# A hybrid recurrent and attention trunk on one core: gates one by one, activations read into place, and two products opened before the last K tile

## The chip, the cores and the metric

The kernel runs on one core of one Trainium2 chip. The metric is the device time of one execution in microseconds (us), the median over the runs; lower is better. A profile shows one execution of its own.

## The reference

The reference is one inference step of a trunk of two layers over 640 tokens: 512 of a prompt and 8 sequences of 16 new ones. Each layer works on a normalised stream, shifted and scaled by a projection of a conditioning vector (adaLN), and adds its output, normalised again and gated, to the stream. Layer 0 is a recurrent mixer, layer 1 attention with stick-breaking weights over a key and value shared by all 16 heads and taken from the stream behind layer 0.

```python
D_MODEL, D_RNN, N_HEADS = 2048, 4096, 16
def recurrent_mixer(hn, h0, conv0, w_in, conv_w, conv_b, w_r, b_r, w_i, b_i, lam, w_out):
    xb, zg = jnp.split(hn @ w_in, 2, axis=-1)
    xb, conv_new = causal_conv(xb, conv0, conv_w, conv_b)
    y, hT = rg_lru(xb, h0, w_r, b_r, w_i, b_i, lam)
    return (y * jax.nn.silu(zg)) @ w_out, hT, conv_new
# rg_lru: r, i = sigmoid(block_diag(x, w_r) + b_r), sigmoid(block_diag(x, w_i) + b_i)
#   log_a = -8 r softplus(-lam); a = exp(log_a); u = sqrt(-expm1(2 log_a)) * (i * x); h = a * h + u
def stick_breaking_mixer(hn, k_all, v_all, w_in, w_out):
    q, zg = jnp.split(hn @ w_in, 2, axis=-1)
    o = stick_breaking(q, k_all, v_all)
    return (o * jax.nn.silu(zg)) @ w_out
# each layer: x = x + gate * rms_norm(out, g_post)
```

## The kernel before, in words

All large products are made in float32 precision out of three passes (`mm3`, L99): each operand is split into a high part (`wh`, `yh`, `xh`, `hh`), made on ScalarE (ACT), and a low part (`wl`, `yl`, ...), made on VectorE (DVE) as the difference; then high × high (L101), low × high (L102) and high × low (L103) go into one bank. The split of a weight is `hilo` (L82): L87 on ACT, L88 on DVE, into three buffers of each (`WB`). The names of the profile follow: `wh<-raw` at L87 is the high part of a weight that was loaded into the buffer `raw`.

The tokens lie along the free axis (640, or two halves of 320), 128 features on the partitions. The program goes through these stages:

- *Start* (`start`, L339). For each of 16 K tiles k of the model dimension: four loads of adaLN weights (`wa`), 16 small products with the conditioning vector into a bank (L223), a copy (`msb`, L225), two products with a selector (L228), then the normalised and modulated K tile k (`hn`), split into `xs` or `xv`; `fill(k - 1)` then multiplies the tile before with the first weights (`wf`) of four output tiles, whose sums stay in the banks `psb` and `pss` ("f banks"): 24 matmuls. K tile 15 is filled behind the loop.
- *Pairs* (`recurrent`, L743). 16 pairs of output tiles of the recurrent dimension. Each pair makes two pair products (`pair_product`, L537): the input branch (`inputs`) and the gate branch (`silu_gates`); those of pair 0 come out of the f banks. A pair product multiplies 14 K tiles in two-by-two blocks in the manner of Strassen's method, with seven sums of activations and seven of weights, called S1, X11, S4, S2, X12, S3, X22 in the order of the code; each is 7 × 3 matmuls of 320 columns (21). The last two K tiles (`PLAIN`) go plainly, 6 matmuls for each quarter. Four banks `pc`, `pa`, `pb`, `pd` take them; `keep` (L559) copies a bank to memory on ACT where its intermediate is needed later; `evac` takes the results out on DVE. Weights come by a generator (`plan`, L442, `pair_weights`, L494): loads on SP into `raw`, `rest`, `sum0`, `sum1` and a small ring `rv`, additions of weight blocks by accumulating loads on POOL, and splits, always three weights ahead (`ahead`, L529).
- *Gates and recurrence* (`lru`, L683), once a pair: four products each for the gate r and the gate i, out of the split activation, into four banks (`psg`), a sigmoid on ACT for each (`g` and `q`), then exp, tanh and sqrt on ACT, the products of them on DVE and a scan. The result goes to memory (`yd`).
- *Two out_products* (`recurrent_out`, L854; `out_product`, L761): 16 K tiles of `yd` each, times `w_out_a`; five token blocks by four column blocks. Weights for two K tiles at a time come into a ring of four buffers, `wr`; the activations come into the same ring (`yr`), are split into `yh` and `yl`, and stay.
- *mid* (L909): residual, norm and transposes, interleaved with the end of the second out_product. `residual` (L840) loads the rows of x into `xx`, in two buffers, and adds them (L851).
- *Shared key and value, 16 heads of attention, out_b*: head after head, with the last product (`attention_begin`, L886, `out_product` again, on `od`) started within the last heads; then the last residual.

Each engine works through its queue in order. A scheduler places the instructions into the queues; `issue_after` ties an instruction behind another, and `high_priority` puts it ahead of others that are ready. So what stands in front of a split on ACT or DVE, and in front of a load on SP, decides when it runs.

## Time and profile before

| | before |
|---|---|
| median of 3 runs | 2911.41 us (2906.17 to 2912.74) |
| the profiled execution | 2916.01 us, of it the span 2914.3 us |
| mean granted clock of TensorE | 0.992 |
| instructions | 48223 |
| TensorE busy | 97% of the span |
| VectorE, ScalarE, GpSimd busy | 68%, 55%, 14% |
| bytes moved by DMA | 536.49 MB, 184 GB/s in the mean |

PE stands for TensorE's matmuls, PEld for its weight loads, DVE for VectorE, ACT for ScalarE, POOL for GpSimd, SP for the engine that issues most loads. A row of a timeline gives the start and the duration in us, the engine, the line of the kernel, the instruction, its output and inputs by the program's names, and in square brackets how long the engine was idle before it and who ended that. Where DVE or ACT is named, the waiting engine waited for that instruction's result. An idle time of TensorE costs what it lasts; an idle time of another engine costs only if TensorE waits for it at the end.

### The profile page before, as it was taken

The page shows a single profiled execution, that of the slowest core. Times are in us where ns is not written, and L with a number is a line of the kernel's source. Part 1 is how long each engine was busy: PE and PEld are TensorE (multiplying, and loading weights), DVE is VectorE, ACT ScalarE, POOL GpSimd, SP SyncE. Part 2 cuts the span into 40 slices and gives each one's busy share as a digit, 9 for nine tenths or more (in the row PEclk, how much of TensorE's full clock was granted, in tenths as well). Part 3 has the DMA queues.
Part 4 walks back from the last instruction along what each step waited for, and adds up shares of the span by engine and source line. Part 5 has one row for each costly group of instructions (what it writes and reads, how often), then busy time and mean ns, then how long its engine had stood idle before and what let it go on. Part 6 is the DMA issues. An engine that isn't in the chain of part 4 may idle for free.

```text
span 2914.3 us, 48223 instructions
## 1 busy us (share of the span) xinstructions
PE 2837.1 (97%) x18784; PEld 2520.8 (86%) x18784; DVE 1977.9 (68%) x2867; ACT 1607.8 (55%) x2464; POOL 420.3 (14%) x589
## 2 busy tenths in 40 slices
PE   6899999999999999999999999999999999999998
PEld 4799999999999977778788999778989999897886
DVE  7677776777677766634568877777666766667335
ACT  5466555655565566533456666674455555546323
POOL 0011222222222200001113322001000000001000
PEclk9899999999999999999999999999999999999999
DMA  9866676667666666555567666663565555656636
GB/s 338 303 143 150 162 163 152 146 164 160 158 146 162 143 195 190 167 147 163 186 209 254 226 209 214 203 200 115 185 197 168 182 175 183 198 169 197 208 109 224
DMA packets 246003, 536.49 MB, mean 184 GB/s; under 512 B 22520, under 2 KB 106616, under 8 KB 244624
## 3 DMA queue, kind: packets, MB, share of 16 engines
q1 hardware_dynamic: 219056, 442.01, 47.7%
q0 software_dynamic: 26720, 91.42, 15.5%
q8 instruction: 147, 2.41, 0.3%
q14 instruction: 80, 0.66, 0.1%
HBM read 496.24 MB, written 37.11 MB: 183 GB/s over the span
## 4 chain that ended last, share of the span: by engine, by line
PE 79%; ACT 6%; DVE 4%; DMA 2%; issue 2%; POOL 0%; DVEq 0%; POOLq 0%; SPq 0%; ACTq 0%
PE acc L101 7%; PE acc L102 7%; PE acc L103 7%; PE psh L101 6%; PE acck L101 5%; PE psh L103 5%; PE psh L102 5%; PE acck L103 5%; PE acck L102 5%; PE pa L101 3%; PE pa L103 3%; PE pa L102 3%; PE psa L198 2%; DVE wl L88 1%; PE pc L101 1%
## 5 line engine op out<-in xcount | busy, mean ns | idle before, releaser
L88 DVE TENSOR_TENSOR wl<-wr,wh 128x1024 fp32r<-128x1024 f32 x216 | 270.3, 1252 | 289.4 <-ACT wh L87 288.1
L87 ACT ACTIVATE wh<-wr 128x1024 fp32r<-128x1024 f32 x216 | 228.2, 1056 | 382.1 <-PE acc L103 228.6
L101 PE MATMUL acc<-wh,yh 128*128 128x512 f32 x960 | 378.8, 395 | 10.3 <-ACT yh L777 5.6
L102 PE MATMUL acc<-wl,yh 128*128 128x512 f32 x960 | 378.3, 395 | 7.7 <-DVE wl L88 7.7
L103 PE MATMUL acc<-wh,yl 128*128 128x512 f32 x960 | 377.0, 394 | 0.3 <-DVE yl L778 0.3
L186 DVE TENSOR_TENSOR wa<-wa,wa 128x1024 bf16<-128x1024 f32 (+1 forms) x256 | 308.6, 1240 | 24.9 <-ACT wa L185 22.7
L101 PE MATMUL psh<-nh,wh 128*128 128x320 f32 x1024 | 323.9, 316 | 0.0
L103 PE MATMUL psh<-nh,wl 128*128 128x320 f32 x1024 | 318.9, 311 | 0.0
L102 PE MATMUL psh<-nl,wh 128*128 128x320 f32 x1024 | 317.4, 310 | 0.0
L185 ACT ACTIVATE wa<-wa 128x1024 bf16<-128x1024 f32 x256 | 263.1, 1052 | 67.2 <-DVE wa L186 46.7
L101 PEld LDWEIGHTS acc<-wh,yh 128*128 128x128 f32 x960 | 182.1, 190 | 58.4 <-issue 8.7
L102 PEld LDWEIGHTS acc<-wl,yh 128*128 128x128 f32 x960 | 182.5, 190 | 47.7 <-DVE wl L88 10.3
L103 PEld LDWEIGHTS acc<-wh,yl 128*128 128x128 f32 x960 | 182.2, 190 | 39.9 <-DVE yl L778 2.2
L101 PEld LDWEIGHTS psh<-nh,wh 128*128 128x128 f32 x1024 | 192.3, 188 | 19.3 <-DVE ql L1112 12.6
L101 PE MATMUL pa<-xs,wh 128*128 128x320 f32 x630 | 194.8, 309 | 0.0
L103 PE MATMUL pa<-xs,wl 128*128 128x320 f32 x630 | 194.7, 309 | 0.0
L102 PE MATMUL pa<-xs,wh 128*128 128x320 f32 x630 | 194.7, 309 | 0.0
L103 PEld LDWEIGHTS psh<-nh,wl 128*128 128x128 f32 x1024 | 192.4, 188 | 0.5 <-DVE wl L88 0.2
L102 PEld LDWEIGHTS psh<-nl,wh 128*128 128x128 f32 x1024 | 192.4, 188 | 0.1
L101 PE MATMUL acck<-nh,wh 128*128 128x320 f32 x512 | 161.5, 315 | 0.0
L481 POOL DMA_DIRECT2D sum<-w_in_a_dram x90 | 79.4, 882 | 559.3 <-DVE wl L88 262.9
L103 PE MATMUL acck<-nh,wl 128*128 128x320 f32 x512 | 158.3, 309 | 0.0
(354 smaller groups left out, 7312.4 us busy)
## 6 DMA issues: line engine op xcount, KB each, us to landing
wa<-w_ada_dram SPq DMA_DIRECT2D x192, 512.0 KB, 4.7
wr<-w_out_a_dram SPq DMA_DIRECT2D x96, 512.0 KB, 4.1
sum<-w_in_a_dram POOLq DMA_DIRECT2D x90, 448.0 KB, 5.6
wr<-w_in_b_dram SPq DMA_DIRECT2D x64, 512.0 KB, 5.3
ck<-cache_k_dram SPq DMA_DIRECT2D x64, 512.0 KB, 6.7
cv<-cache_v_dram SPq DMA_DIRECT2D x64, 512.0 KB, 5.3
wr<-w_out_b_dram SPq DMA_DIRECT2D x56, 512.0 KB, 4.2
raw<-w_in_a_dram SPq DMA_DIRECT2D x60, 448.0 KB, 4.2
```

What stands on the lines that cost most here:

```text
L87: nc.scalar.activation(hi[:, :n], raw, AF.Copy)
L88: nc.vector.tensor_tensor(lo[:, :n], raw, hi[:, :n].bitcast(F32), ALU.subtract)
L101: mm(out, sh, mh, start=start, stop=False, **kw)
L102: mm(out, sh, ml, start=False, stop=False, **kw)
L103: mm(out, sl, mh, start=False, stop=stop, **kw)
L185: nc.scalar.activation(parts[i], raw, AF.Copy)
L186: nc.vector.tensor_tensor(parts[2] if i else raw, raw, parts[i], ALU.subtract)
L198: nc.tensor.matmul(ps[32 * j : 32 * j + 32, :], self.c3[:, 4 * g + j, :], ws[j // 2][i][:, j % 2, :], start=g + i == 0, stop=g == 3 and i ...
L481: self.nc.gpsimd.dma_start(self.big[tag], self.quarter(w, i), accum_op=ALU.add)
```

## The change

**The start.** The loads of the adaLN weights are issued ahead of the rest of each step (`ada_load`). In the last step (k = 15) `fill(14)` comes ahead of the last adaLN products instead of behind them. The two banks that adaLN uses are exchanged. The plan of the weights begins in `start`: the first weights are split before the last K tile is made, and the products S1 and X11 of the first pair product are made (`self.opened`, in banks of the ring `one`) between the last selector products and `fill(15)`. `pair_product` takes over from there (`begun`, `opening`). The first loads of the plan come in another order (`raw`, one small one, `rest`, and `sum1` and two small ones later). `lru_params`, small vectors for the recurrence, is made in step 1 instead of at the end.

**The pairs.** `keep` gets high priority. In `lru` the products go gate by gate: r of both halves of the features, then i of both, and after each the weights of that gate are free for the plan (`ahead(1 - i)`); before, both gates of the first half came first. The four banks are taken by half of the features instead of by gate.

**The out_products.** The activations are loaded straight into the tiles that will hold their low parts (`fetch`, four K tiles at a time, the first four before the first weights) and split in place. They use no buffer of the ring `wr` any more. The splits of the first four have high priority. `kept` says which K tiles are still in memory (the last head's, for out_b).

**mid.** `residual` has six buffers for `xx` instead of two.

The number of matmuls is the same. What the change does to the queues, at three places. First PE's queue at the end of the start; `wa` are adaLN's last weights, `psb` and `pss` with `xv` the fills, `sel` the selector products. Before:

```order
L223 MATMUL pss<-wa_1409,cT 32x256 x4
L223 MATMUL pss<-wa_1415,cT 32x256 x4
L101 MATMUL psb<-xv,wh 128x384
L102 MATMUL psb<-xv,wh 128x384
L103 MATMUL psb<-xv,wl 128x384
L228 MATMUL psb<-sel,msb_1421 128x16 x2
L101 MATMUL pss<-xv,wh 128x256
```

And of the change:

```order
L103 MATMUL pss<-xv,wl 128x256
L228 MATMUL pss<-wa_1433,cT 32x256 x4
L228 MATMUL pss<-wa_1435,cT 32x256 x4
L228 MATMUL pss<-wa_1437,cT 32x256 x4
L228 MATMUL pss<-wa_1439,cT 32x256 x4
L234 MATMUL psb<-sel,msb_1481 128x16 x2
L101 MATMUL pc_1519<-xs,wh 128x320
L102 MATMUL pc_1519<-xs,wh 128x320
L103 MATMUL pc_1519<-xs,wl 128x320
```

`fill(14)` (its last row is the first one here) now ends ahead of the adaLN products, and S1 (`pc`) follows the selector, with X11 (`pa`) and `fill(15)` behind it.

Second, PE's queue in the input branch of a pair, behind S4: the end of the plain products (`pd` with `xv`) and what follows them. Before:

```order
L101 MATMUL pd_3109<-xv,wh 128x320
L102 MATMUL pd_3109<-xv,wh 128x320
L103 MATMUL pd_3109<-xv,wl 128x320
L101 MATMUL pb_3108<-xs,wh 128x320
L102 MATMUL pb_3108<-xs,wh 128x320
L103 MATMUL pb_3108<-xs,wl 128x320
```

And of the change:

```order
L101 MATMUL pd_3107<-xv,wh 128x320
L102 MATMUL pd_3107<-xv,wh 128x320
L103 MATMUL pd_3107<-xv,wl 128x320
L101 MATMUL pa_3022<-xs,wh 128x320
L102 MATMUL pa_3022<-xs,wh 128x320
L103 MATMUL pa_3022<-xs,wl 128x320
```

Before, the first half of X12 (`pb`) followed; now S2 (`pa`) does, whole, and X12 behind it.

Third, ACT's queue at the start of the first out_product, from the last sigmoids of the last pair (`g` and `q` from `psg`) to the first split of `wr`. Before:

```order
L702 ACTIVATE g<-psg_11231,pv 128x320
L702 ACTIVATE g<-psg_11239,pv 128x320
L87 ACTIVATE wh<-wr 128x1024
L702 ACTIVATE q<-psg_11248,pv 128x320
L702 ACTIVATE q<-psg_11256,pv 128x320
L712 ACT_TABLE_LOAD
L712 ACTIVATE q<-g,nk_100 128x640 x2
L716 ACTIVATE g<-g,k_99 128x640 x2
L777 ACTIVATE yh<-yr 128x640
```

And of the change:

```order
L751 ACTIVATE q<-psg_11228,pv 128x320
L751 ACTIVATE q<-psg_11236,pv 128x320
L833 ACTIVATE yh<-yl 128x640 x4
L751 ACTIVATE q<-psg_11246,pv 128x320
L751 ACTIVATE q<-psg_11254,pv 128x320
L763 ACT_TABLE_LOAD
L763 ACTIVATE q<-g,nk_100 128x640 x2
L767 ACTIVATE g<-g,k_99 128x640 x2
L87 ACTIVATE wh<-wr 128x1024
```

Four activations are split in the weight's old place, and the weight in the activation's, behind the tanh.

The diff, cut to its core:

```diff
...
-    def ada_first(self, k, psa, psc, dst):
+    def ada_load(self, k):
+        ws = []
+        for g in range(4):
+            ws.append(self.adap.tile([P, 4, 256], F32, tag="wa", name="wa0", bufs=5))
+            self.nc.sync.dma_start(ws[g], self.I["w_ada0"][k, :, 4 * g : 4 * g + 4, :])
+        return ws
+    def ada_first(self, k, ws, psa, psc, dst):
...
         for g in range(4):
-            ws = self.adap.tile([P, 4, 256], F32, tag="wa", name="wa0", bufs=5)
-            nc.sync.dma_start(ws, self.I["w_ada0"][k, :, 4 * g : 4 * g + 4, :])
             for j in range(4):
-                last = nc.tensor.matmul(psa[32 * j : 32 * j + 32, :], self.cT[:, 4 * g + j, :], ws[:, j, :], start=False, stop=g == 3, **kw)
+                last = nc.tensor.matmul(psa[32 * j : 32 * j + 32, :], self.cT[:, 4 * g + j, :], ws[g][:, j, :], start=False, stop=g == 3, **kw)
         m = self.adap.tile([P, 256], F32, tag="msb0", name="msb0", bufs=2)
         nc.scalar.activation(m, psa, AF.Copy)
...
         for i in range(2):
...
         self.ada_put(psc, dst)
         return last.ins
...
             g, s = gs[:, k, :], sh[:, k, :]
-            last = self.ada_first(k, spare[1][:, 256:], spare[0][:, FIRST : FIRST + 32], [self.ada_dst(0, part, k, o) for part, o in ((1, gs), (0, sh))])
+            end = k == KD - 1
+            dst = [self.ada_dst(0, part, k, o) for part, o in ((1, gs), (0, sh))]
+            ada = lambda: self.ada_first(k, ws, spare[0][:, 256:], spare[1][:, FIRST : FIRST + 32], dst)
+            ws = self.ada_load(k)
+            if end:
+                with self.tc.issue_after(last):
+                    last = fill(k - 1)
+                with self.tc.issue_after(last):
+                    last = ada()
+            else:
+                last = ada()
             if k == 0:
...
             self.hT.append((hh, hl))
-            if k > 0:
+            if 0 < k and not end:
                 with self.tc.issue_after(last):
...
             nc.sync.dma_start(raw, self.I["w_first"][:, 4 * P * k : 4 * P * k + 4 * P])
+            if end:
+                self.planned, self.ready = self.plan(), []
+                self.ready.append(next(self.planned))
             wt[k] = self.hilo(raw, P)
+            if k == 1:
+                self.lru_params(rp)
             if k % 2 == 0:
...
                 self.combine(rp, slot, even, tmp)
-        self.lru_params(rp)
-        fill(KD - 1)
+        self.ready.append(next(self.planned))
+        with self.tc.issue_after(last):
+            self.opened = [self.bank(n)[:, :HALF] for n in ("pc7", "pa7")]
+            for ps, i in zip(self.opened, (S1, X11)):
+                last = self.seven(ps, i, True)
+        with self.tc.issue_after(last.ins):
+            fill(KD - 1)
         self.begun = dict(units)
...
         self.smalls = []
-        for _ in range(3):
-            self.small_load()
         at = [w[q] for q in order] + [None, None]
-        for tag, n in (("raw", 0), ("rest", 2), ("sum1", 1)):
-            self.big_load(tag, at[tag == "sum1"], n)
+        self.big_load("raw", at[0], 0)
+        self.small_load()
+        self.big_load("rest", at[0], 2)
         for i, q in enumerate(order):
-            yield from self.pair_weights(*at[i : i + 3], *("sum0", "sum1", "sum0")[i % 2 : i % 2 + 2])
+            weights = self.pair_weights(*at[i : i + 3], *("sum0", "sum1", "sum0")[i % 2 : i % 2 + 2])
+            if i == 0:
+                yield from islice(weights, 2)
+                self.big_load("sum1", at[1], 1)
+                for _ in range(2):
+                    self.small_load()
+            yield from weights
             if q == 1 or q > 16:
...
-    def pair_product(self, ep, evac):
-        nc = self.nc
+    def seven(self, ps, i, first):
+        hi, lo = self.weights()
+        c = slice(HALF * i, HALF * i + HALF)
+        for n, x in enumerate(self.pairs):
+            last = self.mm3(ps, hi[:, n, :], lo[:, n, :], x[:, 0, c], x[:, 1, c], first and n == 0, n == NP - 1, skip_group_check=True)
+        return last
+    def keep(self, ps, tag="keep", bufs=2):
+        t = self.ep.tile([P, HALF], F32, tag=tag, name=tag, bufs=bufs)
+        with self.tc.high_priority(200):
+            self.nc.scalar.activation(t, ps, AF.Copy)
+        return t
+    def opening(self):
+        c, a = self.opened
+        return c, a, self.keep(c, "keep5", 1), self.keep(a)
+    def pair_product(self, evac, begun=None):
         kw = dict(skip_group_check=True)
+        keep = self.keep
...
         def seven(ps, i, first):
-            hi, lo = self.weights()
-            c = slice(HALF * i, HALF * i + HALF)
-            for n, x in enumerate(self.pairs):
-                self.mm3(ps, hi[:, n, :], lo[:, n, :], x[:, 0, c], x[:, 1, c], first and n == 0, n == NP - 1, **kw)
+            self.seven(ps, i, first)
             self.ahead()
...
-        def keep(ps, tag="keep", bufs=2):
-            t = ep.tile([P, HALF], F32, tag=tag, name=tag, bufs=bufs)
-            nc.scalar.activation(t, ps, AF.Copy)
-            return t
-        c, a = bank("pc7"), bank("pa7")
-        seven(c, S1, True)
-        p5 = keep(c, "keep5", 1)
-        seven(a, X11, True)
-        p1 = keep(a)
+        if begun is None:
+            c, a = bank("pc7"), bank("pa7")
+            seven(c, S1, True)
+            p5 = keep(c, "keep5", 1)
+            seven(a, X11, True)
+            p1 = keep(a)
+        else:
+            c, a, p5, p1 = begun
         seven(c, S4, False)
...
-            self.pair_product(ep, evac)
+            self.pair_product(evac, begun)
         return pv, rows
...
         gate_bank = lambda n: self.half(n, "psg2") if n < 2 else self.bank("psg2")
-        rs, qs = [], []
-        for h in range(2):
-            pv = pv2[:, h, :]
-            fs = slice(P * h, P * h + P)
-            g = []
-            for i in range(2):
-                hi, lo = gw[i]
+        gates, qs = [], []
+        for i in range(2):
+            hi, lo = gw[i]
+            for h in range(2):
+                pv = pv2[:, h, :]
+                fs = slice(P * h, P * h + P)
                 v = ep.tile([P, T], F32, tag="gq"[i], name="gq"[i], bufs=2)
                 for c in range(2):
-                    ps = gate_bank((2 * i + c) % 4)[:, :HALF]
+                    ps = gate_bank(2 * h + c)[:, :HALF]
                     s = slice(HALF * c, HALF * c + HALF)
...
                     last = A.activation(v[:, s], ps, AF.Sigmoid, bias=pv[:, 5 + i : 6 + i])
-                g.append(v)
-            rs.append(g[0])
-            V.tensor_tensor(xf[h], g[1], xf[h], ALU.mult)
-        self.ahead()
+                if i:
+                    V.tensor_tensor(xf[h], v, xf[h], ALU.mult)
+                else:
+                    gates.append(v)
+            self.ahead(1 - i)
+        rs = gates
...
         self.ep = ep
-        self.planned, self.ready = self.plan(), []
+        begun = self.opening()
         self.ahead()
...
         for j in range(16):
-            first = self.inputs(1, ep) if j == 0 else None
+            first = self.inputs(1, ep, begun) if j == 0 else None
             zs = self.silu_gates(j, ep)
...
-    def out_product(self, src, w, chunks, evac, fill=iter(())):
-        nc = self.nc
-        ys, slots = [], []
+    def out_product(self, src, w, chunks, evac, fill=iter(()), kept=()):
+        nc = self.nc
+        ys, raws = [], []
+        def fetch(k):
+            hi, lo = (self.hp.tile([P, 4, T], F32R, tag="h", name=n) for n in ("yh", "yl"))
+            for kk in range(k, k + 4):
+                yh, yl = hi[:, kk - k, :], lo[:, kk - k, :]
+                if kk not in kept:
+                    nc.sync.dma_start(yl.bitcast(F32), src[P * kk : P * kk + P, :])
+                raws.append((yh, yl))
         def load(k):
-            nonlocal slots
-            if k % 4 == 0:
-                slots = [self.hp.tile([P, 4, T], F32R, tag="h", name=n) for n in ("yh", "yl")]
-            yh, yl = (x[:, k % 4, :] for x in slots)
-            if k in self.local:
-                raw = self.local[k]
-            else:
-                raw = self.wp.tile([P, self.WW], F32, tag="wr", name="yr", bufs=self.RB)[:, :T]
-                nc.sync.dma_start(raw, src[P * k : P * k + P, :])
-            self.last_split = nc.scalar.activation(yh, raw, AF.Copy).ins
-            nc.vector.tensor_tensor(yl, raw, yh.bitcast(F32), ALU.subtract)
+            if k % 4 == 0 and len(raws) < 16:
+                fetch(len(raws))
+            yh, yl = raws[k]
+            raw = self.local[k] if k in kept else yl.bitcast(F32)
+            with self.tc.high_priority(200 if k < 4 else 0):
+                self.last_split = nc.scalar.activation(yh, raw, AF.Copy).ins
+                nc.vector.tensor_tensor(yl, raw, yh.bitcast(F32), ALU.subtract)
             ys.append((yh, yl))
+        fetch(0)
         for c, (toks, n) in enumerate(chunks):
...
-        return self.out_product(self.od, self.I["w_out_b"], chunks, gate)
+        return self.out_product(self.od, self.I["w_out_b"], chunks, gate, kept=(NHEAD - 1,))
...
             ts = slice(P * t, P * t + P)
-            ch = self.residual(t, oacc, ss, self.I["x"][ts, :], bp, 2)
+            ch = self.residual(t, oacc, ss, self.I["x"][ts, :], bp, 6)
             nc.gpsimd.dma_start(self.x1d[ts, :], oacc[t])
...
```

22 lines of the change are left out of this document (13 added, 9 removed).

## The prediction

> **What bounds the kernel now.** First the page: which engine fills the span.
>
> ```profile
> span 2914.3 us, 48223 instructions
> PE 2837.1 (97%) x18784; PEld 2520.8 (86%) x18784; DVE 1977.9 (68%) x2867; ACT 1607.8 (55%) x2464; POOL 420.3 (14%) x589
> ```
>
> TensorE (PE) is the bound: 2914.3 − 2837.1 = 77.2 us without a matmul. The change takes no matmul away, so all that it can win is idle time of PE and matmuls run at a low clock. I read where both lie from the table of windows (stretch, its length, busy time of each engine, granted clock, DMA share):
>
> ```profile
> 0.00:130.00 130.00, 102.24 (x910) 77.67 (x914) 92.95 (x257) 65.40 (x115) 3.00 (x8) 0.97 0.93 336
> 130.00:157.00 27.00, 21.87 (x129) 19.82 (x122) 15.34 (x53) 11.11 (x23) 3.18 (x7) 0.81 0.66 166
> 157.00:232.00 75.00, 72.19 (x481) 70.26 (x480) 59.30 (x93) 54.78 (x82) 12.79 (x20) 1.00 0.64 144
> 288.00:1000.00 712.00, 700.84 (x4720) 692.33 (x4720) 528.82 (x829) 428.57 (x642) 160.00 (x230) 1.00 0.68 157
> 1039.00:1056.00 17.00, 11.43 (x43) 8.86 (x42) 14.07 (x22) 14.13 (x19) 0.49 (x1) 0.80 0.25 73
> 1267.00:1281.00 14.00, 8.97 (x33) 6.62 (x32) 3.70 (x4) 3.75 (x5) 0.00 (x0) 0.88 0.45 142
> 1447.00:1461.00 14.00, 10.91 (x36) 8.39 (x35) 10.78 (x13) 7.48 (x16) 4.42 (x4) 0.76 0.89 311
> 2670.00:2685.00 15.00, 11.85 (x44) 8.19 (x43) 14.99 (x22) 9.06 (x16) 5.33 (x4) 0.77 0.48 165
> ```
>
> The first 130 us lose 27.8 us beside DMA engines that are 93% busy, and the change leaves them alone. In the order of the rows, idle after that is 5.1 (end of the start stage), 2.8 (first pairs), 11.2 (pairs), 5.6 (start of the first out_product), 5.0 (start of the second), 3.1 (mid), 3.2 (start of out_b). Six of these are one wait or a few; the pairs are thirteen equal ones. The rows of PE's timeline name them (start, duration, instruction, idle before it and who ended it):
>
> ```profile
> 132.13 0.64 PE L223 MATMUL pss<-wa,cT 128*32 128x256 f32 x8 [1.60 <-DMA wa<-w_ada_dram]
> 142.86 0.44 PE L101 MATMUL psb<-xv,wh 128*128 128x384 f32 x1 [1.55 <-ACT xv L384]
> 149.79 0.41 PE L101 MATMUL pc<-xs,wh 128*128 128x320 f32 x1 [1.30 <-ACT hb L624]
> 288.90 0.42 PE L103 MATMUL pb<-xs,wl 128*128 128x320 f32 x1 [0.85 <-DVE wl L88]
> 1046.35 0.79 PE L101 MATMUL acc<-wh,yh 128*128 128x512 f32 x1 [5.57 <-ACT yh L777]
> 1273.54 0.76 PE L101 MATMUL acc<-wh,yh 128*128 128x512 f32 x2 [4.53 <-ACT wh L87]
> 1274.80 0.80 PE L102 MATMUL acc<-wl,yh 128*128 128x512 f32 x1 [0.50 <-DVE wl L88]
> 1452.31 0.79 PE L102 MATMUL acc<-wl,yh 128*128 128x512 f32 x1 [3.09 <-DVE wl L88]
> 2678.22 1.22 PE L102 MATMUL acc<-wl,yh 128*128 128x512 f32 x2 [2.74 <-DVE wl L88]
> ```
>
> Two corrections to these idle times. First, rows of a matmul overlap, as these two show, the first and the last of 19 in a row:
>
> ```profile
> 1037.84 0.31 PE L103 MATMUL psg<-xh,wl 128*128 128x320 f32 x1
> 1040.48 0.30 PE L103 MATMUL psg<-xh,wl 128*128 128x320 f32 x1
> ```
>
> The pitch is (1040.48 − 1037.84)/18 = 0.147 us, the row lasts 0.31; so a stall costs its idle time and 0.16 more. Second, the clock. Before and after the wait at 1449:
>
> ```profile
> 1448.16 0.39 PE L101 MATMUL acc<-wh,yh 128*128 128x512 f32 x1
> 1448.38 0.39 PE L102 MATMUL acc<-wl,yh 128*128 128x512 f32 x1
> ...
> 1453.76 0.63 PE L102 MATMUL acc<-wl,yh 128*128 128x512 f32 x1
> 1454.19 0.63 PE L103 MATMUL acc<-wh,yl 128*128 128x512 f32 x1
> ```
>
> The pitch goes from 0.22 to 0.43: half clock. What it takes from a window is length × (1 − clock): 14 × 0.24 = 3.4 us at 1447, as much at 1039 and 2670 (17 × 0.20, 15 × 0.23), 14 × 0.12 = 1.7 at 1267, 27 × 0.19 = 5.1 at 130. A wait of 3 us is thus worth 6.
>
> [...]
>
> **The change part by part.**
>
> *A, the end of the start.* Fill(14) now stands ahead of the last adaLN products, and 42 products of the first pair (S1 and X11, 7 × 3 each) stand ahead of fill(15). ACT's rows:
>
> ```profile
> 134.12 0.38 ACT L225 ACTIVATE msb<-pss 128x256 f32<-128x256 f32 x1 [4.67 <-PE pss L223]
> 141.23 0.95 ACT L87 ACTIVATE wh<-raw 128x896 fp32r<-128x896 f32 x1 [3.42 <-PE pss L102]
> ```
>
> Before, fill(14) starts when the last weights have come, and the chain that makes K tile 15 (msb, hn, xv, from 134.1) is held 3.4 us by a weight split that waits for fill(14)'s slot; xv comes behind that split and ends PE's wait at 142.86. Now fill(14) fills the wait for the last weights (1.60 and what is left of it): 24 matmuls of 384 and 256 columns, 320 in the mean, some 24 × 0.147 = 3.5 us. The chain, without the 3.42, needs about 142.86 − 3.42 − 134.12 = 5.3 us; 42 × 0.147 = 6.2 us cover it. So the 5.1 of idle and the 5.1 of clock are both open to be won. Against it: S1 and X11 were the cover of the evacuation of the f banks (the hb row at 149.79) and of the next splits; with them gone only S4 and the plain product, (21 + 12) × 0.147 = 4.9 us, stand between fill(15) and S2, and ACT has two copies of banks and the hb rows ahead of S2's split: a new stall of 0 to 3. Also msb stands behind the raw split on ACT, whose DMA competes with the last adaLN loads (0.93 busy). I take 7 of 10.2, with 3 to 10 as bounds. If the cover of the chain failed altogether, its 5.3 us would be open.
>
> *A2, the first pairs.* The 2.8 us idle until 232 are waits of the kind treated next, in an order not yet regular: 1.5, bounds 0 and 3.
>
> *B, the pairs.* 712 − 700.84 = 11.16 us are 13 waits of 0.86, like the one at 288.90. Who is late, from DVE's and ACT's timeline:
>
> ```profile
> 286.29 1.55 DVE L728 SCALAR_TENSOR_TENSOR g<-g,q 128x640 f32<-128x640 f32 x2
> 287.76 1.08 DVE L88 TENSOR_TENSOR wl<-raw,wh 128x896 fp32r<-128x896 f32 x1
> 289.57 0.42 ACT L561 ACTIVATE keep<-pa 128x320 f32<-128x320 f32 x1
> ```
>
> The matmul that waits is the third of X12, whose low part is made at 287.76 to 288.84, behind two gate operations. X12 stands there early, ahead of S2, because S2's bank is kept only at 289.57, behind the gates' roots. In the new order keep goes first, S2 follows the plain products (its weights are long split), and X12 comes 21 × 0.147 = 3.1 us later. 0.86 is less than 3.1, so the wait goes: 13 × (0.86 + 0.16) = 13.3 us. What could be late next: with the gates one by one the four i products use the banks that the r products just left, and ACT has a weight split (0.95, as in the raw row) between their sigmoids: up to 0.25 in each pair. I take −1.3 for that: 12, bounds 6 (the wait halved) and 13.3.
>
> *C, the first out_product.* ACT's rows before:
>
> ```profile
> 1039.49 1.05 ACT L87 ACTIVATE wh<-wr 128x1024 fp32r<-128x1024 f32 x1
> 1041.39 1.28 ACT L712 ACT_TABLE_LOAD   x1
> 1042.69 1.55 ACT L712 ACTIVATE q<-g,nk 128x640 f32<-128x640 f32 x2
> 1044.14 1.53 ACT L716 ACTIVATE g<-g,k 128x640 f32<-128x640 f32 x2
> 1045.58 0.72 ACT L777 ACTIVATE yh<-yr 128x640 fp32r<-128x640 f32 x1
> ```
>
> Before, the weight is split early and the activation waits behind exponentials and tanh. Now it is the other way round: four activations early, in the weight's place, and the weight behind the tanh. Four splits in place of one weight's add 4 × 0.72 − 1.05 = 1.8 us ahead of the exponentials, so the tanh, which made room at 1045.6, does so at 1047.4; the weight's high part ends at 1048.4 and its low part 1.2 later (the wl row in E), at 1049.6. Before, the first low-part product came one pitch of half clock behind 1046.35, at 1046.8. So some 2.8 us more stall: −3, bounds −4 and +1 (if the four splits fit where ACT waits for the gates anyway). The half clock stays.
>
> *D, the second out_product.* Its activations came through the weights' own ring of buffers:
>
> ```profile
> 1271.80 0.74 ACT L777 ACTIVATE yh<-yr 128x640 fp32r<-128x640 f32 x1 [3.96 <-DMA yr<-yd]
> ```
>
> ACT idles 3.96 for one of them and the weight split (1272.45) comes right behind. With the activations loaded into tiles of their own, four rows ahead, neither waits for the other's buffer: 4.53 + 0.50 + 0.16 of stall and 1.7 of clock, 6.9 in all. The first weights still need a slot that the products before free: 6, bounds 4 and 7.
>
> *E, mid.* DVE's rows:
>
> ```profile
> 1448.42 0.75 DVE L851 SCALAR_TENSOR_TENSOR oacc<-oacc,ss,xx 128x512 f32<-128x512 f32 x1 [2.37 <-DMA xx<-x_dram]
> 1451.04 1.22 DVE L88 TENSOR_TENSOR wl<-wr,wh 128x1024 fp32r<-128x1024 f32 x1
> ```
>
> The low part waits on DVE behind residual steps that wait for x, in two buffers. Six buffers let x come early. The stall, 3.25, and its 3.4 of clock, less 0.35 of half clock that ran inside the wait: 6.3. DVE is busy 10.8 of these 14 us, so a rest of 1 may stay: 5.5, bounds 3 and 6.5.
>
> *F, start of out_b.* Its wait is for a low part as well, behind this:
>
> ```profile
> 2666.62 4.15 DVE L1126 RECIPROCAL ez<-ez 128x640 f32<-128x640 f32 x1
> ```
>
> In the new order that split stands ahead of the reciprocal, which delays the chain by 1.2, and the next split comes later, behind the scans. The loads of the activations stand together on SP, where weights' loads queue behind them. The wait moves, I think, more than it goes: 0, bounds −1.5 and +1.5.
>
> The sum: 7 + 1.5 + 12 − 3 + 6 + 5.5 + 0 = 29. The profiled execution took 2916.01 us (span 2914.3 and 1.7 around it), so it would take 2887; it lies 4.6 above the median of the runs, and from the median 2911.4 the same 29 give 2882.4.
>
> **Rivals.**
>
> *R1, the pairs keep a wait.* With X12 moved, the next low part or the i gates' banks are late by about as much as X12 was; DVE's rows at 286 to 289 are gapless, which speaks for it, the 3.1 us of slack against it. B gives 2 in place of 12: gain 19, 2892.
>
> *R2, the start gives nothing.* The start is bound by DMA until 134, and the plan's first loads now compete there; S2 waits for what S1 and X11 covered. A gives 0 for 7: gain 22, 2889. For it: 0.93 in the first window; against: 0.66 in the second.
>
> *R3, the out_products lose.* All three start with weights behind the activations, on SP and on ACT, and the stalls that D should win return there with half clock; C −4, D 0, F −3: gain 19, 2892.
>
> *R4, slower.* Keep now has priority on ACT and waits there for its product; the weight splits queued behind it wait too. There are 32 pair products (two in each of 16 pairs). The split and its low part take 0.95 + 1.08 = 2.0; if keep pushed one of them past its product by s each time, the loss is 32 s, against 17 gained elsewhere (29 − 12). It decides from s = 0.53. At s = 1.0 the sum is −15: 2926. Against it: one product is 3.1 us and the ring holds three weights, so a split may be late by more than a product.
>
> *R5, the clock does not come back.* If low clock were not tied to waits of 2 to 4 us, the idle time would go and the clock's share stay: E −3.4, D −1.7, A −3: gain 21, 2890. Against it: every window with such a wait has the low clock, and the windows without one stand at 1.00. [...]
>
> **How the numbers follow.** Forecast 0.60; R1 0.14, R2 0.09, R3 0.10, R4 0.05, R5 0.02. The bounds of the terms add up to gains of 10.5 and 42; R1, R2, R3 and R5 lie within. I take some 2 more on the far side: gains of 11 to 44, 2867 to 2900, which leaves out R4 and the mixtures of rivals. A measurement can tell 0.2%, some 6 us (the three runs shown spread by 6.6). Forecast, R1, R2, R3 and R5 together have 0.95 and are faster by more, less 0.04 for three of them at once: 0.91; same 0.05 (that, and the mild end of R4); slower 0.04.
>
> **What would show it.** A: no wait longer than 1 us between 130 and 150, clock near 1.0 there, and a wait of at most 2 ahead of S2. B: the window of the same pairs with idle under 3 us and DVE's low part of X12 done before PE asks. C: a first stall of 7 to 9 us that ends on the weight, not on the activation. D, E: windows at full clock without a wait over 1 us. F: a stall of 2 to 4 us. I am wrong if the pairs still show thirteen equal waits, or if the out_products and mid still run at half clock at their start.

## The result and the profile after

The changed kernel takes 2887.86 us in the median (2886.3 to 2894.29, 4 runs) against 2909.06 of the kernel before (2906.17 to 2912.74, 4 runs): ratio 0.9927, 95% interval 0.9906 to 0.9947. That is 21 us less, where 29 were forecast; the time lies inside the range. The profiled execution of after took 2894.29 us, of before 2916.01, so the two traces differ by 21.7 us as well. One of the ten executions of the experiment inplace_alone took 9193 us, and its ratio leaves that one out.

The page of after, the lines that answer to those of before:

```profile
span 2892.6 us, 48123 instructions
PE 2826.5 (98%) x18784; PEld 2515.8 (87%) x18784; DVE 1966.0 (68%) x2865; ACT 1609.6 (56%) x2464; POOL 412.0 (14%) x589
```

The same number of matmuls; PE's busy time falls by 10.6 us (in part because matmuls at half clock are longer, 0.63 us for a row of 512 columns against 0.39 in the kernel before, and the mean granted clock rose from 0.992 to 0.994), and its idle time from 77.2 to 66.1. By stage, the windows of after, in the order of before's and moved by what was won up to there (the last three columns are the granted clock, the DMA share and GB/s):

```profile
0.00:130.00 130.00, 100.79 (x888) 76.56 (x889) 94.83 (x283) 66.59 (x117) 3.00 (x8) 0.96 0.91 333
130.00:157.00 27.00, 25.52 (x192) 24.18 (x192) 16.47 (x31) 14.38 (x28) 4.17 (x8) 1.00 0.83 207
157.00:232.00 75.00, 72.22 (x486) 70.94 (x485) 59.24 (x96) 54.33 (x81) 12.86 (x19) 1.00 0.61 145
288.00:1000.00 712.00, 712.00 (x4810) 705.26 (x4809) 535.89 (x841) 437.83 (x650) 158.34 (x240) 1.00 0.68 158
1018.00:1035.00 17.00, 9.52 (x36) 7.40 (x35) 14.31 (x23) 16.59 (x23) 0.00 (x0) 0.70 0.87 324
1247.00:1261.00 14.00, 14.00 (x64) 11.59 (x63) 1.23 (x1) 2.85 (x4) 0.00 (x0) 1.00 0.51 199
1419.00:1433.00 14.00, 11.34 (x48) 8.43 (x47) 10.39 (x13) 6.86 (x13) 5.92 (x5) 1.00 1.01 376
2642.00:2671.00 29.00, 21.41 (x120) 15.08 (x118) 24.77 (x33) 21.56 (x39) 6.78 (x5) 0.82 0.61 202
```

The pairs (fourth row) have no idle time at all now, the second out_product (sixth) neither, at full clock. The first pairs (third) idle as before. The first out_product (fifth) has 7.5 us idle, where there were 5.6, mid (seventh) still 2.7, and the start of out_b (last) idles 7.6 us. The waits that are left, from PE's timeline:

```profile
1027.96 1.65 PE L101 MATMUL acc<-wh,yh 128*128 128x512 f32 x3 [7.44 <-ACT wh L87]
1421.98 0.50 PE L102 MATMUL acc<-wl,yh 128*128 128x512 f32 x1 [0.90 <-DVE sr L289]
1426.43 0.50 PE L102 MATMUL acc<-wl,yh 128*128 128x512 f32 x1 [1.41 <-DVE wl L88]
2649.42 1.06 PE L1270 MATMUL zc<-ck,qs 128*32 128x512 f32 x8 [2.40 <-DVE e L1207]
2652.83 0.80 PE L103 MATMUL acc<-wh,yl 128*128 128x512 f32 x1 [2.34 <-DVE yl L834]
2663.53 0.66 PE L1290 MATMUL pas<-ident,e 128*128 128x128 f32 x4 [2.29 <-ACT e L1208]
```

Where the time came from is read from seven points that both programs pass, the starts of matmuls on PE in the two traces (us; the difference between two gains is what a stage gives):

| point | before | after | gained up to here |
|---|---|---|---|
| first gate product of pair 0 | 175.1 | 168.1 | 7.0 |
| first gate product of pair 2 | 269.4 | 262.4 | 7.0 |
| first gate product of pair 15 | 1033.6 | 1013.3 | 20.3 |
| first matmul of the first out_product | 1046.35 | 1027.96 | 18.4 |
| last matmul of the second out_product | 1517.4 | 1489.3 | 28.1 |
| last psh product (queries of the last head) | 2664.4 | 2637.0 | 27.4 |
| last matmul | 2904.3 | 2882.7 | 21.7 |

By stage: start 7.0, first pairs 0, pairs 13.3, first out_product's start −1.9, both out_products with mid 9.7, attention −0.7, out_b −5.8.

### The profile page after: what moved, and what is told of

Same layout as the page of the kernel before. It is cut to its first block, busy times and chain, and to the rows that moved or that the text cites. A ratio compares the mean times of both kernels' runs of the same rounds, so it can differ in the third digit from the quotient of the medians.

```text
span 2892.6 us, 48123 instructions
## 1 busy us (share of the span) xinstructions
PE 2826.5 (98%) x18784; PEld 2515.8 (87%) x18784; DVE 1966.0 (68%) x2865; ACT 1609.6 (56%) x2464; POOL 412.0 (14%) x589
## 4 chain that ended last, share of the span: by engine, by line
PE 87%; DVE 2%; DMA 2%; ACT 1%; issue 1%; POOL 0%; SPq 0%; DVEq 0%; POOLq 0%; ACTq 0%
PE acc L101 7%; PE acc L103 7%; PE acc L102 7%; PE psh L101 5%; PE acck L101 5%; PE psh L103 5%; PE acck L102 5%; PE psh L102 5%; PE acck L103 5%; PE pa L101 3%; PE pa L103 3%; PE pa L102 3%; PE pc L103 2%; PE pc L101 2%; PE pc L102 2%; PE psa L198 2%
## 5 line engine op out<-in xcount | busy, mean ns | idle before, releaser
L102 PE MATMUL acck<-nl,wh 128*128 128x320 f32 x512 | 158.3, 309 | 0.0
```

The lines of the kernel that those rows point to most:

```text
L102: mm(out, sh, ml, start=False, stop=False, **kw)
```

## The experiments

Twelve kernels ran; the ratio is always to the kernel before, with runs of it on the same chip, the interval behind it. The medians of the kernel before beside the experiments lie between 2904.0 and 2908.4 us, so a difference of a few us between the medians of two experiments is not shown by them alone; the stages are. The experiments' own points are read from one trace of each, as in the table above.

**The pairs: keep, or the gates?** Two kernels do one part each, on the kernel before.

```diff
 def keep(ps, tag="keep", bufs=2):
-    nc.scalar.activation(t, ps, AF.Copy)
+    with self.tc.high_priority(200):
+        nc.scalar.activation(t, ps, AF.Copy)
```

> The kernel before with one edit: the copies of banks (keep) get high priority; the gates stay as they were. My theory (the wait for X12's low part comes from the place of keep in ScalarE's queue, gates order has no part in it): the thirteen waits of 0.86 us between 288 and 1000 us are gone, the period of a pair falls from 58.78 to about 57.75 us, and the last gate product of pair 15 ends some 13 us earlier than before; the total falls by 13 us. Rival (the wait goes only when each gate's weights are freed by itself): the period stays at 58.78 us, or falls by less than 0.4, and the total falls by less than 5.

2890.36 us, ratio 0.9943 (0.9928 to 0.9958): 18 us less, of which the pairs show 14.3. The window of the pairs:

```profile
288.00:1000.00 712.00, 712.00 (x4816) 706.29 (x4815) 538.09 (x844) 434.92 (x650) 146.35 (x242) 1.00 0.67 159
```

No idle time; from pair 2's gates to pair 15's it takes 749.9 us, against 764.2 before and 750.9 in the changed kernel. One edit of one line makes all of the pairs' gain.

```diff
-        for h in range(2):
-            for i in range(2):
+        for i in range(2):
+            for h in range(2):
...
-                    ps = gate_bank((2 * i + c) % 4)[:, :HALF]
+                    ps = gate_bank(2 * h + c)[:, :HALF]
...
-        self.ahead()
+            self.ahead(1 - i)
```

> The kernel before with one edit: the gates one by one, with their weights freed apart; keep has no priority. My theory: X12 still stands ahead of S2 on TensorE, so a wait for a low part of 0.5 to 1.5 us stays in each pair and the total moves by less than 5 us either way. Rival (the gates' order makes the gain): the pairs' waits are gone and the total falls by about 13 us.

2965.96 us, ratio 1.0204 (1.0189 to 1.0219): 57.5 us slower, far from both expectations. That a wait stays in each pair is my theory's; its size, and that the total rises by more than 5 us, nobody expected. The window, and PE's and ACT's rows of one pair:

```profile
288.00:1000.00 712.00, 677.93 (x4387) 666.01 (x4387) 490.50 (x761) 401.44 (x591) 137.83 (x217) 0.96 0.61 145
```

```profile
280.16 0.41 PE L101 MATMUL pb<-xs,wh 128*128 128x320 f32 x1 [2.17 <-ACT wh L87]
281.76 0.64 PE L103 MATMUL pb<-xs,wl 128*128 128x320 f32 x1 [1.05 <-DVE wl L88]
283.26 0.47 PE L101 MATMUL pc<-xs,wh 128*128 128x320 f32 x1
283.53 0.47 PE L102 MATMUL pc<-xs,wh 128*128 128x320 f32 x1
```

```profile
279.17 0.93 ACT L87 ACTIVATE wh<-raw 128x896 fp32r<-128x896 f32 x1
280.01 0.72 ACT L725 ACTIVATE g<-g 128x640 f32<-128x640 f32 x1
281.47 0.42 ACT L561 ACTIVATE keep<-pc 128x320 f32<-128x320 f32 x1
281.79 0.43 ACT L561 ACTIVATE keep<-pa 128x320 f32<-128x320 f32 x1
```

Without keep's priority the new gate order lets the scheduler place X12 (`pb`) ahead even of S4, since both copies of banks come behind the gates' roots (L725) on ACT. X12's weight is split late (279.17), so PE waits 2.17 and 1.05 us in a pair, and half clock follows (pitch 0.27 at 283 in place of 0.147): the mean clock of the window is 0.96. The stretch of thirteen pairs takes 825.6 us, 61 more. So the gates' part, alone, is the worst of the change, and beside keep it costs 1.0 us in thirteen pairs (750.9 to 749.9). Neither of these two stretches has idle time in the window shown, so what the 1.0 us goes into stays open.

**The out_products in place.** On the kernel before, the new `out_product` alone:

```diff
+        def fetch(k):
+            hi, lo = (self.hp.tile([P, 4, T], F32R, tag="h", name=n) for n in ("yh", "yl"))
+            for kk in range(k, k + 4):
...
+                    nc.sync.dma_start(yl.bitcast(F32), src[P * kk : P * kk + P, :])
```

> The kernel before with one edit: the activations of the out_products read into place, in all three of them. My theory: the first out_product's stall grows from 5.57 us to 7.5 to 8.5 and ends on the weight; the second one's (4.53 and 0.50) goes with its half clock, some 6 us; the start of out_b, from the first scores of the last head to the end, loses 5 to 6 us, as in the changed kernel; total about 1 to 3 us slower than before or no change. Rival (the start of out_b loses for another reason, the other stages' timing): out_b's part stays within 1.5 us of before and the total falls by 3 to 5 us.

2906.94 us, ratio 0.9994 (0.9984 to 1.0005): no change that can be told. Its parts are near my theory's: from the first gate product of pair 15 to the first out_product 14.64 us instead of 12.77, no wait at the second out_product, and out_b, from the last psh product to the last matmul, 244.4 us instead of 239.9 (a loss of 4.5, where 5 to 6 were expected). The four kernels with the old out_b took 239.3 to 240.3 there. What D wins, C and F give back.

**The start alone.** The new start, with the old gates, keep, out_product and xx; against the changed kernel:

```diff
-        with self.tc.high_priority(200):
-            self.nc.scalar.activation(t, ps, AF.Copy)
+        self.nc.scalar.activation(t, ps, AF.Copy)
...
-            ch = self.residual(t, oacc, ss, self.I["x"][ts, :], bp, 6)
+            ch = self.residual(t, oacc, ss, self.I["x"][ts, :], bp, 2)
```

and `lru` and `out_product` as they stand in the kernel before.

> The kernel before with the start's edits alone (fill of tile 14 ahead of the last adaLN products, S1 and X11 ahead of the fill of tile 15, the plan's order, the vectors of the recurrence made early); no priority for keep, gates as before. My theory: the third pair's gates come 7 us earlier than before, as in the changed kernel (269.4 to 262.4), and the pairs' period stays at 58.78; total 7 us less. Rival (part of the start's gain needs keep's priority): the third pair's gates come less than 5 us earlier.

2903.5 us, ratio 0.9995 (0.9984 to 1.0005), though the median of before beside it was 2908.4: the total doesn't show the expected 7 us. The first gate product of pair 0 comes at 166.4 us. But three kernels with the old start (keep_alone, gates_alone, inplace_alone) have it at 171.2, 168.3 and 171.3, and only the profiled execution of before at 175.1. The windows of the first two beside it:

```profile
130.00:157.00 27.00, 24.12 (x180) 22.28 (x179) 21.14 (x62) 16.70 (x30) 4.04 (x8) 1.00 0.69 183
```

```profile
130.00:157.00 27.00, 22.91 (x155) 21.72 (x156) 21.04 (x60) 15.83 (x29) 4.07 (x8) 1.00 0.68 165
```

Full clock in both, where the prediction's window had 0.81. So the start has less to win than one trace of before showed: nine kernels with the new start lie between 165.1 and 168.1 (mean 166.6), four with the old between 168.3 and 175.1 (mean 171.5), and the difference of the means is 4.9 us. Part of that is when the weights arrived. Counted from the landing of the last adaLN weights in each trace, the first gate product comes 33.5 to 35.0 us later in the nine (mean 34.4), 37.1 to 38.6 in the three others with the old start (mean 37.7) and 41.7 in the trace of before, with its half clock. At full clock the new start is thus worth some 3.3 us.

**Is fill(14)'s new place worth anything?** On the changed kernel, put back behind the adaLN products.

```diff
+                with self.tc.issue_after(last):
+                    last = ada()
                 with self.tc.issue_after(last):
                     last = fill(k - 1)
-                with self.tc.issue_after(last):
-                    last = ada()
```

> The changed kernel with one edit: the fill of tile 14 stands behind the last adaLN products again, as before; S1 and X11 still stand ahead of the fill of tile 15. My prediction held that the fill in the wait for the last weights covers 2.2 us. Theory 1 (it does not: the fill itself waits about 1 us for its activations, lasts longer than that wait and pushes the last adaLN products back, from about 133 to 136 us): with the fill behind, the last adaLN products come at 132 to 134 us, the first gate product of pair 0 at 165 to 168 us, no later than with the change, and the total is within 3 us of the changed kernel. Theory 2 (the cover is worth what I gave it): the first gate product comes 2 us later or more, 168.5 or above, and the total rises by 2 us or more.

2890.33 us, ratio 0.9954 (0.9937 to 0.997), 2.5 us above the changed kernel's median and inside its spread. In its trace the last adaLN products come at 129.9 and the first gate product of pair 0 at 163.2, the earliest of all. Its window:

```profile
130.00:157.00 27.00, 27.00 (x191) 26.65 (x184) 16.92 (x34) 16.88 (x31) 3.31 (x7) 1.00 0.78 198
```

No idle time there, so theory 1's part on the trace holds: the two opened products do the work, and fill(14)'s new place isn't needed for it. Counted from the landing of the last adaLN weights, the first gate product comes at 33.6 us here, and at 33.5 to 35.0 in the nine kernels with the fill ahead: the new place gains nothing there. Whether it costs a us, one trace can't tell.

**out_b: through the ring, or without the priority.** Both on the changed kernel. First, out_b's activations through the ring again (`ring_product` is the old `out_product`, called for out_b alone).

```diff
-        return self.out_product(self.od, self.I["w_out_b"], chunks, gate, kept=(NHEAD - 1,))
+        return self.ring_product(self.od, self.I["w_out_b"], chunks, gate)
```

> The changed kernel with one edit: out_b takes its activations through the ring of the weights again, as before; the two out_products of the recurrent layer stay in place. My theory: from the last psh product to the last matmul it takes 239.4 to 240.3 us as in the runs with the old out_b, not 245.7 as in the changed kernel; total 5 to 6 us less than the changed kernel. Rival (the loss at the start of out_b comes with an earlier stage's timing): this stretch stays above 243 us.

2888.33 us, ratio 0.9937 (0.9922 to 0.9952). The stretch takes 242.0 us: the waits are the old ones again (0.41 and 2.74), with 1.10, 0.72, 0.84 and 0.59 more in the next 25 us. Between theory and rival, nearer the theory; the total doesn't show it.

```diff
-            with self.tc.high_priority(200 if k < 4 else 0):
+            with self.tc.high_priority(200 if k < 4 and not kept else 0):
```

> The changed kernel with one edit: in out_b the first four activations are split without high priority. Theory 1 (the priority puts a weight split and four splits ahead of the last head's chain, whose reciprocal starts 2.45 us late): the stretch from the last psh product to the last matmul falls from 245.7 to 241 to 243 us. Theory 2 (the loads of the activations come late behind others on SP and hold ScalarE's queue, whatever the priority): it stays within 1 us of 245.7.

2885.52 us, ratio 0.9931 (0.9917 to 0.9946); the stretch takes 239.1 us: theory 1, and a little more than it expected. The total, 2.3 us below the changed kernel's, doesn't show it by itself. Before, ACT copied the last head's gate 0.35 us behind the start of the last psh product:

```profile
2664.79 0.44 ACT L1119 ACTIVATE z<-psh 128x320 f32<-128x320 f32 x1 [1.29 <-PE psh L103]
```

In the changed kernel, ACT's rows and the reciprocal of the last head on DVE:

```profile
2637.92 0.74 ACT L833 ACTIVATE yh<-yl 128x640 fp32r<-128x640 f32 x1 [1.45 <-DMA yl<-od]
2638.57 0.42 ACT L1176 ACTIVATE z<-psh 128x320 f32<-128x320 f32 x1
2638.88 1.05 ACT L87 ACTIVATE wh<-wr 128x1024 fp32r<-128x1024 f32 x1
2639.83 0.73 ACT L1181 ACTIVATE ez<-z 128x640 f32<-128x640 f32 x1
```

```profile
2639.96 1.22 DVE L88 TENSOR_TENSOR wl<-wr,wh 128x1024 fp32r<-128x1024 f32 x1 [0.31 <-ACT wh L87]
2641.63 4.15 DVE L1183 RECIPROCAL ez<-ez 128x640 f32<-128x640 f32 x1
```

A split that waits 1.45 us for its load stands ahead of the copy of the last head's gate, and a weight's split ahead of its exponential, on ACT and on DVE. The reciprocal starts 2641.63 − 2637.00 = 4.6 us behind the last psh product; before it was 2666.62 − 2664.44 = 2.2. Without the priority (last psh product at 2635.1):

```profile
2638.79 4.16 DVE L1183 RECIPROCAL ez<-ez 128x640 f32<-128x640 f32 x1
```

3.7 us behind, with a split still waiting for a load ahead of it, but not the weight; and PE's waits from there on are 1.93, 2.74 and 0.88 instead of 2.40, 2.34 and 2.29 with 0.56. What the priority was for (the first activations early) the program has anyway. A single trace says too much here as well: the six kernels with this out_b and the priority take 240.2 to 245.7 us for the stretch (mean 243.3), so the changed kernel's is the longest of them. The three without the priority (this one and the last two below) take 237.8 to 239.1, and their reciprocal starts 2.8 to 3.7 us behind the last psh product instead of 4.3 to 5.3.

**The first out_product: the weight first.**

```diff
-                hi, lo = self.wsplit(w[n, :, k : k + 2, :], 512)
+                with self.tc.high_priority(200 if c == k == 0 and not kept else 0):
+                    hi, lo = self.wsplit(w[n, :, k : k + 2, :], 512)
```

> The changed kernel with one edit: the load and the split of the first out_product's first weights get high priority (those for out_b not). My theory (the stall of 7.44 us is the weight's split behind exp and tanh, and the half clock of 10.24 us follows from it): the stall falls below 2 us, a new one of 1 to 3 us comes at the second pair of K tiles, whose split is still behind the tanh; 5 to 9 us less from the last gate product to the end of the first out_product. Rival (the activations are not there any earlier, since their buffers come free only when the pair products end): the stall ends on an activation and stays above 5 us.

2878.67 us, ratio 0.9911 (0.9896 to 0.9926), 9 us below the changed kernel's median; by the ratios (0.9911 and 0.9927) it is less, and their intervals overlap. The stage shows it. ACT's rows in the changed kernel and here:

```profile
1019.23 2.60 ACT L833 ACTIVATE yh<-yl 128x640 fp32r<-128x640 f32 x4
1023.98 1.55 ACT L763 ACTIVATE q<-g,nk 128x640 f32<-128x640 f32 x2
1025.43 1.53 ACT L767 ACTIVATE g<-g,k 128x640 f32<-128x640 f32 x2
1026.87 1.04 ACT L87 ACTIVATE wh<-wr 128x1024 fp32r<-128x1024 f32 x1
```

```profile
1012.84 1.06 ACT L87 ACTIVATE wh<-wr 128x1024 fp32r<-128x1024 f32 x1
1015.26 1.40 ACT L833 ACTIVATE yh<-yl 128x640 fp32r<-128x640 f32 x2
1017.04 1.59 ACT L833 ACTIVATE yh<-yl 128x640 fp32r<-128x640 f32 x2 [0.39 <-DMA yl<-yd]
```

The product starts 7.04 us behind the first gate product instead of 14.64, without a wait and without half clock (the pitch of its rows is 0.23 us from the first on); the second weights, as expected, are 1.13 and 0.69 us late:

```profile
1025.61 1.43 PE L101 MATMUL acc<-wh,yh 128*128 128x512 f32 x5 [1.13 <-ACT wh L87]
1027.73 0.50 PE L102 MATMUL acc<-wl,yh 128*128 128x512 f32 x1 [0.69 <-DVE wl L88]
```

The same with the first two weights:

```diff
-                with self.tc.high_priority(200 if c == k == 0 and not kept else 0):
+                with self.tc.high_priority(200 if c == 0 and k < 4 and not kept else 0):
```

> The changed kernel with one edit: the loads and splits of the first out_product's first two weights get high priority. My theory: as with the first alone, and the wait at the second pair of K tiles goes too: 7 to 10 us less than the changed kernel. Rival (the second split, ahead of the gates' sigmoids, holds the gates' banks or the activations): a new stall of 1 to 3 us among the gates or ahead of the first product, and no more than 5 us less.

2879.4 us, ratio 0.9903 (0.9887 to 0.992). The wait at the second weights goes, and one of 1.42 us for a low part of an activation comes at the third: no better than the first alone.

**mid: two, six, twelve buffers for x.** On the changed kernel, two instead of six:

```diff
-            ch = self.residual(t, oacc, ss, self.I["x"][ts, :], bp, 6)
+            ch = self.residual(t, oacc, ss, self.I["x"][ts, :], bp, 2)
```

> The changed kernel with one edit: two buffers for x in mid instead of six, as before. My prediction gave the six buffers 5.5 us; my theory now (the loads of x stand on SP between weights' loads that wait for their buffers, with two as with six): the waits in mid are 2 to 3.5 us together, as in the changed kernel (0.90 and 1.41), and the total moves by less than 3 us. Rival (the six buffers do win what was predicted): a wait of 3 us or more with half clock behind it, the total 5 us above the changed kernel.

2892.03 us, ratio 0.995 (0.9932 to 0.9968). The waits are 0.85, 1.72 and 1.42, together 4.0 against 2.3 with six, at full clock in both (a pitch of 0.23 us behind each wait); but from the first matmul of the out_products to their last it takes 461.7 us and with six 461.4, so theory, not rival, though the waits and the total are both somewhat above what the theory allowed. The total's 4 us more lie elsewhere or in the spread. Other traces say the same of this stretch: 462.3 us with two buffers (inplace_alone), 459.7 to 462.2 with six (the changed kernel, fill_behind, outb_ring, outb_noprio). Why six don't help: SP's queue and DVE's row in the changed kernel.

```profile
1404.20 0.33 SPq L96 DMA_DIRECT2D wr<-w_out_a_dram  x1
1405.91 0.99 SPq L904 DMA_DIRECT2D xx<-x_dram  x2
1407.70 0.33 SPq L96 DMA_DIRECT2D wr<-w_out_a_dram  x1
1408.37 0.99 SPq L904 DMA_DIRECT2D xx<-x_dram  x2
1410.83 0.33 SPq L96 DMA_DIRECT2D wr<-w_out_a_dram  x1
```

```profile
1420.04 0.75 DVE L908 SCALAR_TENSOR_TENSOR oacc<-oacc,ss,xx 128x512 f32<-128x512 f32 x1 [2.74 <-DMA xx<-x_dram]
```

Six tiles are there early, for one and a half token blocks; the others' loads come one or two at a time, between weights' loads, while the DMA engines are full (1.01 in the window above).

**All three places together.** First the two out_products' edits on the changed kernel:

```diff
-            with self.tc.high_priority(200 if k < 4 else 0):
+            with self.tc.high_priority(200 if k < 4 and not kept else 0):
...
-                hi, lo = self.wsplit(w[n, :, k : k + 2, :], 512)
+                with self.tc.high_priority(200 if c == k == 0 and not kept else 0):
+                    hi, lo = self.wsplit(w[n, :, k : k + 2, :], 512)
```

> The changed kernel with two edits: the first out_product's first weights with high priority, and out_b's first activations without. If the two places are independent: the stall at the first out_product about 1 us and at the second weights 2, and the stretch from the last psh product to the last matmul near 239 us; total 2872 to 2877. Rival (what is won at one place is lost at the other): not below 2878.

2876.83 us, ratio 0.9904 (0.9889 to 0.9919), 11 us below the changed kernel's median: the out_b stretch takes 237.8 us, the start of the first out_product 7.04. The two places are independent, and the total is at the upper edge of what was expected. With twelve buffers for x besides:

```diff
-            ch = self.residual(t, oacc, ss, self.I["x"][ts, :], bp, 6)
+            ch = self.residual(t, oacc, ss, self.I["x"][ts, :], bp, 12)
```

> As both_fixed, and with twelve buffers for x in mid, enough for the three token blocks of the first group, so that all their loads are issued at the start of the second out_product. My theory (x's loads between the weights' loads make the residual wait, and the weights' low parts wait behind it on VectorE): the waits on DMA at the residual of the first group are gone, the waits in mid fall below 1 us, and it takes 2 to 5 us less than both_fixed. Rival (VectorE is simply full there): the waits stay at 2 us or more.

2875.02 us, ratio 0.9895 (0.988 to 0.9909), the fastest of all: 13 us below the changed kernel, 30 below the kernel before. mid's window and what is left of its wait:

```profile
1410.00:1424.00 14.00, 12.95 (x55) 9.89 (x54) 8.91 (x10) 6.99 (x12) 4.28 (x5) 1.00 0.95 381
```

```profile
1420.61 0.51 PE L102 MATMUL acc<-wl,yh 128*128 128x512 f32 x1 [0.76 <-DVE wl L88]
```

From the first matmul of the out_products to the last it takes 459.7 us; both_fixed took 465.1, with a wait of 3.29 in it. With twelve, no residual step on DVE waits for a load of x; in both_fixed two did, 0.76 and 4.45 us. In total the two differ by 1.8 us, less than the expected 2 to 5, and their intervals overlap. Nor is 465.1 what six buffers usually cost: the waits in mid add up to 2.0 to 3.4 us in the seven traces with six, and 3.29 is near the upper end. That the wait goes is seen in one trace; how much time that wins is not shown.

## Why the prediction was right, and where not

The direction and the range hold; the forecast was 8 us too good. Term by term, from the seven points:

| term | forecast | measured | |
|---|---|---|---|
| A, start | 7 | 7.0 in these two traces, 4.9 in the means, 3.3 from the weights' landing | right by luck of the trace |
| A2, first pairs | 1.5 | 0.0 | wrong |
| B, pairs | 12 | 13.3 | right |
| C, first out_product | −3 | −1.9 | right |
| D and E, second out_product and mid | 11.5 | 9.7 in these two traces | D right here, less against other traces; E too large |
| F, start of out_b | 0, bounds ±1.5 | −5.8 in these two traces, −3.4 in the means | outside its bounds |

*B* is shown: the wait came from keep's place on ACT, which put X12 ahead of S2; the priority alone removes it (keep_alone). "I take −1.3 for that", for the gates' banks, was 1.0, but no wait for the banks is seen, so that is the size and not the working. R1, that the pairs keep a wait, is ruled out by the window without idle time, and so is R4 here: with the priority no split was pushed past its product. How near a slow case lay, gates_alone shows: it needs only the gates without the priority. R2 is out too, by the 3.3 us of the start, and so is R5: where the waits went, at the second out_product and in mid, the clock of the windows is 1.00.

*C* went as worked out, the weight behind the tanh. The stall grew by 1.9 rather than 2.8, since the four splits took 2.60 us, not 2.88, and PE's first three products (1027.96, x3) need no low part of the weight.

*A* failed as a working, though its number came out. Its clock share, "the 5.1 of clock", belonged to the one profiled execution: the three others with the same start had full clock there (1.00 in the window of each). And "fill(14) fills the wait for the last weights" was not so: the last adaLN products came at 137.8 us instead of 133.7, since the fill itself waited for its activations and lasted longer than the wait for the weights; PE's row in the changed kernel:

```profile
132.56 0.44 PE L101 MATMUL psb<-xv,wh 128*128 128x384 f32 x1 [0.97 <-ACT xv L403]
```
What won is the opening. From the last adaLN products to the first gate product it took 36.9 to 37.9 us in the three kernels with the old start that ran at full clock, and 33.3 in fill_behind, which has the opening and the fill in its old place. In the changed kernel it is 30.3, but there the fill has already run ahead of those products, and they come later by about as much.

*A2* failed at "waits of the kind treated next", which counted them as gone with nothing in their place. The waits for X12 did go (0.57, 0.99 and 0.57 before), but others of the same sum came: two of the changed kernel's four waits there (1.22 and 0.76) are for a keep on ACT itself, as one of before's (0.68) was, and two (0.68 and 0.53) are for other low parts. The first of them:

```profile
200.28 0.42 PE L101 MATMUL pa<-xv,wh 128*128 128x320 f32 x1 [1.22 <-ACT keep L584]
```

From pair 0's gates to pair 2's it takes 94.3 us in every trace, with every order.

*D* was sized from the profiled execution, 4.53 and 0.50 with half clock (0.88 over the window). Other kernels with the old ring waited 3.85 (keep_alone), 2.17 and 0.53 (gates_alone), or 1.97 and 0.53 (start_alone). In the two traces it gave 6.9 (the wait went, and the clock of the window rose from 0.88 to 1.00); against the three others, from the 600th to the 900th matmul of the out_products, the changed kernel gains 6.0, 3.3 and 3.1, so over the four traces D is worth 4.8 in the mean. The 6.9 leave 2.8 for *E*. There the failed step is "Six buffers let x come early": by xx_undone six are worth 0.3 us against two, since loads still wait on SP and in the full DMA engines (a share of 1.01). The wait of 3.09 us with 3.4 us of clock, from which E was sized, was that of one execution: keep_alone, also with two buffers, waited 0.39, 1.04 and 1.38, and xx_undone 0.85, 1.72 and 1.42 at full clock. With twelve buffers the wait is all but gone in the one trace there is.

*F* is the largest miss: "The wait moves, I think, more than it goes". I had seen the weight's split ahead of the reciprocal and counted 1.2 us against a wait won elsewhere. What I had not counted is that the high priority of the first four activations holds the copy of the last head's gate behind a load on ACT, too, so that everything behind it, the scores, the scans and the sums, waited one after another (2.40, 2.34, 2.29, 0.56). Part of the −5.8 belongs to the one trace: the stretch has a mean of 243.3 us in the six kernels with this out_b and the priority, and of 239.9 in the four with the old one. R3 named the place and a price of −3 for F, near the −3.4 of these means; it was half right, as D did win.

That the prediction took the clock of one execution at its face value (5.1 us in *A*, "a wait of 3 us is thus worth 6" in *E*) oversized both; the last section shows why.

## What to carry to other kernels

A copy of a bank that a later product waits for belongs ahead of elementwise work in an in-order queue, and its place decides what the scheduler puts next on TensorE (X12 before, with a wait of 0.86 us in each pair; S2 in keep_alone, with none): one priority was worth more than the rest of the change (14.3 us in the pairs, of some 21). High priority for one consumer is paid by whoever stood in that queue (at out_b 3.4 us in the means); look there for the next critical chain before giving it. Size a term from several executions when it rests on a DMA wait or on the clock.

## What the runs showed of the hardware

The same wait is not always followed by the same loss of clock. The wait of 2.74 us at the start of out_b is the same in the kernel before and in keep_alone; the windows of 14 us around it are not:

```profile
2674.00:2688.00 14.00, 10.59 (x40) 7.08 (x40) 13.40 (x22) 8.42 (x15) 6.16 (x5) 0.76 0.56 169
```

```profile
2652.00:2666.00 14.00, 9.95 (x40) 6.36 (x32) 12.96 (x21) 8.11 (x14) 6.15 (x5) 0.88 0.55 176
```

14 × 0.24 = 3.4 us lost in the one, 14 × 0.12 = 1.7 in the other. What sets the size of the loss is not shown. With two sizes behind one wait, a clock loss read from one trace is one draw.

In these traces a wait behind a DMA varied where the code is the same, and one behind an engine's own work did not. The wait at the second out_product, for a weight's split that stood behind a load of activations, was 4.53, 3.85, 2.17 and 1.97 us in four kernels with the same code there (before, keep_alone, gates_alone, start_alone). The one at the first out_product, behind the exponentials and tanh, was 5.57 in the kernel before and 7.44 in the changed one; inplace_alone, whose out_product is the changed kernel's, took the same 14.64 us from the first gate product of pair 15 to the start of the product.
